# RMSNorm with SiLU on one core: five loads and 174 semaphore increments ahead of the entry barrier, and a scratch transfer on ScalarE's queue

## The chip, the core and the metric

The kernel runs on one core of a Trainium2 chip. A core has TensorE (PE), VectorE (DVE), ScalarE (ACT), GpSimd (POOL) and SyncE (SP), each with an instruction stream of its own, and 16 DMA engines that move data between the chip's memory (HBM, "DRAM" in the code) and the on-chip memory SBUF. The metric is device microseconds of one execution. The kernel before takes 161.42 us, the median of three runs (161.13 to 161.73).

## The reference

```python
batch, seq, dim = 16, 1024, 512          # x: float32, 33.6 MB; gamma: ones(512); eps: 1e-5
rms = np.sqrt(np.mean(x ** 2, axis=-1, keepdims=True) + eps)
x_norm = x / rms * gamma
return (x_norm * (1.0 / (1.0 + np.exp(-x_norm)))).astype(np.float32)
```

There are 16,384 rows of 512 numbers. Each row is divided by its root mean square, multiplied by gamma and passed through SiLU. 33.55 MB are read and 33.55 MB are written.

## The kernel before

**Tiling.** The rows lie over 128 partitions, 128 rows for each. They are computed in place in `xb`, a ring of 100 rows for each partition, in 32 chunks of `cn = 4` rows. The 128 rows are cut into 12 loads and 11 stores, given as (first row, rows): the loads are (0,4), (4,4), (8,8), five of 16 rows, (96,4), (100,12), (112,12) and (124,4); the stores are (0,16), (16,8), (24,8), four of 16 rows, (96,4), (100,12), (112,8) and (120,8). A load or store of n rows moves one run of n x 2 KB for every partition, so 4 rows are 8 KB runs, 1 MB in all.

**The DMA order.** All loads (L121) and stores (L127) are issued by SyncE, in an order written out by hand: nine loads, which fill the ring, then three stores, then the last three loads, then eight stores. The last three loads reuse the ring's first 28 rows, so each waits for the semaphore of a store. A store waits on `s_swish` until its chunks are computed. At the end SyncE waits (L238) for the stores that nothing has waited for yet.

**The entry barrier.** The framework puts a block ahead of the kernel body (L255 in the profile): GpSimd fills four constants, every engine executes a DRAIN, and all meet at a barrier of semaphores. Two more such rounds follow (L66, where the tile context is closed). The kernel takes the first `early = 2` loads out of the body and inserts them into SyncE's entry stream ahead of its DRAIN, so that the transfers start while the engines still meet.

**One chunk.** ScalarE waits for the chunk's load (L167), squares two rows with a running sum (L170, each followed by an instruction that reads the accumulator), and squares the other two into PSUM (L177). VectorE sums these two (L205). GpSimd adds eps (L151) and raises to the power -0.5 (L158). VectorE multiplies four rows by that and by gamma (L216). ScalarE applies SiLU in place to the four rows (L189), two chunks after it squared them.

**Gamma.** GpSimd clears `gamma4` (L146), ScalarE issues a DMA (L193) that puts gamma into one partition of each quarter, ScalarE loads its activation table (L196), and VectorE spreads gamma over the partitions (L229).

Of the kernel before, what the change touches and what calls it, by code (L numbers as in the profile page):

```python
# [9 lines left out]
def kernel(  # L10
# [7 lines left out]
    nc = tc.nc  # L18
    P = nc.NUM_PARTITIONS
    AF = mybir.ActivationFunctionType  # L20
    ALU = mybir.AluOpType
    fp32 = mybir.dt.float32
# [12 lines left out]
    order += [("store", t) for t in range(3)]  # L35
    order += [("load", i) for i in range(loads.index((100, 12)), len(loads))]
    order += [("store", t) for t in range(3, len(stores))]
    early = 2
    cn = 4
    n_sq = 2  # L40

# [26 lines left out]
    def sbuf(name, shape, dt=fp32):  # L68
        return nc.alloc_sbuf_tensor(name, shape, dt).ap()
# [10 lines left out]

    ld = [nc.alloc_semaphore(f"ld{t}") for t in range(len(loads))]
    st = [nc.alloc_semaphore(f"st{t}") for t in range(len(stores))]
    s_gld = nc.alloc_semaphore("s_gld")
    s_zero = nc.alloc_semaphore("s_zero")
    s_half = nc.alloc_semaphore("s_half")
# [9 lines left out]
    def need(ins, sem, value):  # L95
        return ins.wait_op(sem, value, "sem-ge")

    def dram(ap, piece):
        a, n = piece
        g = max(g for g in range(len(groups)) if first[g] <= a)  # L100
        r = a - first[g]
        assert r + n <= groups[g], piece
        rows = ap[P * first[g] : P * (first[g] + groups[g])]
        return rows.rearrange("(p n) d -> p n d", n=groups[g])[:, r : r + n, :]

    def buf(piece):
        a, n = piece
        at = a % ring
        assert at + n <= ring, piece
        return xb[:, at : at + n, :]  # L110
# [3 lines left out]
    def load(i):  # L114
        a, n = loads[i]
        for u, (c, m) in enumerate(stores):
            over = c + ring < a + n and a < c + m + ring
            if over and u not in stored_by_sync:
                nc.sync.wait_ge(st[u], 16)
                stored_by_sync.add(u)  # L120
        return nc.sync.dma_start(  # L121
            out=buf(loads[i]), in_=dram(xf, loads[i])
        ).then_inc(ld[i], 16)

    def store(t):
        need(
            nc.sync.dma_start(out=dram(of, stores[t]), in_=buf(stores[t])),  # L127
            s_swish, ends[t],
        ).then_inc(st[t], 16)

    entry = nc.main_func.blocks[0].instructions
    here = nc.cur_bb.bb.instructions
    for t in range(early):
        ins = load(t).ins
        assert here[-1] is ins or here[-1].name == ins.name
        here.pop()
        at = next(
            i for i, other in enumerate(entry)
            if other.engine == mybir.EngineType.SP
            and isinstance(other, mybir.InstDrain)  # L140
        )
        entry.insert(at, ins)
    for what, t in order[early:]:
        load(t) if what == "load" else store(t)

    nc.gpsimd.memset(gamma4, 0.0).then_inc(s_zero, 1)  # L146
    nc.gpsimd.memset(neg_half, -0.5).then_inc(s_half, 1)  # L147
    nc.gpsimd.wait_ge(s_half, 1)
    for k in range(K):
        need(  # L150
            nc.gpsimd.tensor_scalar(  # L151
                out=aeps[:, k, :], in0=ms[:, k, :], scalar1=eps_f, scalar2=None,
# [6 lines left out]
                out=rstd[:, k, :], in0=aeps[:, k, :], in1=neg_half, op=ALU.pow  # L159
# [25 lines left out]
    def swish(k):  # L185
# [3 lines left out]
            nc.scalar.activation(out=rows, in_=rows, func=AF.Silu), s_norm, k + 1  # L189
        ).then_inc(s_swish, 1)  # L190

    need(
        nc.scalar.dma_start(out=gamma4[0:P:32, :], in_=gamma.partition_broadcast(4)),  # L193
        s_zero, 1,
# [79 lines left out]
```

## Time and profile before

| | before |
|---|---|
| median of 3 runs | 161.42 us (161.13 to 161.73) |
| the profiled execution | 161.94 us, of which the profile's span is 160.6 us |
| busy DVE, ACT, POOL | 124.5, 129.6, 65.4 us |
| SyncE's DMA queue (q1) | 67.11 MB, 98.1% of 16 engines' span |
| ScalarE's DMA queue (q10) | 8 packets, 0.01 MB |
| instruction queue (q14) | 4 packets in the span, 0.03 MB |
| last store | issued at 140.45 us, landed at 160.58 us |

The span runs from the first instruction of the program (SyncE's first load, at 0.00) to its last (SyncE's last wait); the 1.3 us between the span and the execution's time lie outside the program. The profile lists the engines' instructions; SyncE's loads and stores are shown by the instant at which they are issued, and the 16 DMA engines that carry them have rows of their own. Besides the instructions, the trace holds a record of every DMA packet (queue, start, duration, size) and of every increment of a semaphore; where a time below is given from these records, it says so.

### The profile page before, as it was taken

The numbers are of one execution on the slowest core, as the hardware profiler recorded it, in microseconds if no ns is written. First come the engines' busy times: TensorE is split into PE (matmuls) and PEld (weight loads), VectorE is DVE, ScalarE is ACT, GpSimd is POOL, SyncE is SP. The second block draws the span as 40 slices with busy tenths as digits, with TensorE's granted clock in tenths as the row PEclk, the third lists the DMA queues.
The fourth block names the chain that finished last, engine by engine and source line by source line (L and its number), as shares of the span: only waits on it lengthen the run. The fifth ranks groups of instructions, "written<-read, shape, count | busy, mean of one in ns | idle before, by whom it ended". The sixth has DMA issues, their size and how long they took to land.

```text
span 160.6 us, 503 instructions
## 1 busy us (share of the span) xinstructions
DVE 124.5 (78%) x162; ACT 129.6 (81%) x193; POOL 65.4 (41%) x70
## 2 busy tenths in 40 slices
DVE  0287959999999999999999999999999999400000
ACT  1939959999999999999999999999999994700000
POOL 1053545555555555555555555555555555000000
DMA  7999999999999999999999999999999999899993
GB/s 263 449 465 392 498 416 392 481 432 392 453 449 400 424 404 369 459 424 392 426 453 447 410 435 433 435 465 408 424 475 408 400 490 416 369 451 437 428 420 139
DMA packets 3324, 67.15 MB, mean 418 GB/s; under 512 B 372, under 2 KB 372, under 8 KB 376
## 3 DMA queue, kind: packets, MB, share of 16 engines
q1 hardware_dynamic: 3312, 67.11, 98.1%
q14 instruction: 4, 0.03, 0.0%
q10 hardware_dynamic: 8, 0.01, 0.0%
HBM read 33.56 MB, written 33.55 MB: 418 GB/s over the span
## 4 chain that ended last, share of the span: by engine, by line
ACT 63%; DMA 12%; issue 7%; DVE 4%; SPq 0%; ACTq 0%
ACT xb L189 25%; ACT junk L170 22%; ACT sq L177 16%; DMA xb<-in_x_dram 12%; DVE xb L216 3%; DVE ms L205 1%; SPq L121 0%; ACTq L167 0%
## 5 line engine op out<-in xcount | busy, mean ns | idle before, releaser
L216 DVE SCALAR_TENSOR_TENSOR xb<-xb,rstd,gamma_sb 128x512 f32<-128x512 f32 x128 | 87.3, 745 | 0.0
L189 ACT ACTIVATE xb<-xb 128x2048 f32<-128x2048 f32 x32 | 60.9, 1903 | 2.8 <-DVE xb L216 2.8
L205 DVE TENSOR_REDUCE ms<-sq 128x2 f32<-128x1024 f32 x32 | 39.2, 1225 | 14.0 <-ACT sq L177 10.6
L151 POOL TENSOR_SCALAR aeps<-ms 128x4 f32<-128x4 f32 x32 | 20.6, 645 | 65.6 <-DVE ms L205 65.6
L158 POOL TENSOR_TENSOR rstd<-aeps,neg_half 128x4 f32<-128x4 f32 x32 | 44.0, 1376 | 2.7
L170 ACT ACTIVATE junk<-xb 128x512 f32<-128x512 f32 x64 | 37.2, 582 | 4.5 <-DMA xb<-in_x_dram 4.5
L177 ACT ACTIVATE sq<-xb 128x1024 f32<-128x1024 f32 x32 | 32.2, 1005 | 0.0
L170 ACT ACTIVATION_READ_ACCUMULATOR junk<-xb 128x1 f32 x64 | 11.9, 186 | 0.0
L196 ACT ACT_TABLE_LOAD x1 | 1.3, 1283 | 3.6 <-issue 3.6
L146 POOL MEMSET gamma<- 128x512 f32 x1 | 0.5, 525 | 1.5 <-POOLq L66 1.5
L229 DVE STREAM_SHUFFLE gamma_sb<-gamma 128x512 f32<-128x512 f32 x1 | 0.7, 720 | 0.0
L255 POOL MEMSET const-float32-0.0<- 128x1 f32 x1 | 0.1, 99 | 0.2 <-issue 0.2
L255 POOL MEMSET const-bfloat16-1.0<- 128x1 bf16 x1 | 0.1, 102 | 0.0
L255 POOL MEMSET const-uint8-127<- 128x1 uint8 x1 | 0.1, 102 | 0.0
L147 POOL MEMSET neg_half<- 128x4 f32 x1 | 0.1, 102 | 0.0
L255 POOL MEMSET const-float32-1.0<- 128x1 f32 x1 | 0.1, 98 | 0.0
L229 DVE LOAD_MASK_SELECT gamma_sb<-gamma x1 | 0.0, 15 | 0.0
## 6 DMA issues: line engine op xcount, KB each, us to landing
xb<-in_x_dram SPq DMA_DIRECT2D x5, 4096.0 KB, 38.5
out_dram<-xb SPq DMA_DIRECT2D x5, 4096.0 KB, 36.3
out_dram<-xb SPq DMA_DIRECT2D x4, 2048.0 KB, 30.2
xb<-in_x_dram SPq DMA_DIRECT2D x2, 3072.0 KB, 18.2
xb<-in_x_dram SPq DMA_DIRECT2D x4, 1024.0 KB, 12.3
out_dram<-xb SPq DMA_DIRECT2D x1, 3072.0 KB, 25.0
xb<-in_x_dram SPq DMA_DIRECT2D x1, 2048.0 KB, 10.2
out_dram<-xb SPq DMA_DIRECT2D x1, 1024.0 KB, 29.7
```

The costliest lines, as they stand in the source:

```text
L146: nc.gpsimd.memset(gamma4, 0.0).then_inc(s_zero, 1)
L147: nc.gpsimd.memset(neg_half, -0.5).then_inc(s_half, 1)
L151: nc.gpsimd.tensor_scalar(out=aeps[:, k, :], in0=ms[:, k, :], scalar1=eps_f, scalar2=None, op0=ALU.add,),
L158: nc.gpsimd.tensor_tensor(out=rstd[:, k, :], in0=aeps[:, k, :], in1=neg_half, op=ALU.pow),
L170: acc = nc.scalar.activation(out=junk[n % 2], in_=xb[:, at + j, :], func=AF.Square, scale=inv_d**0.5, accum_out=ms[:, k, j : j + 1],)
L177: square = nc.scalar.activation(out=sq[k % 2], in_=xb[:, at : at + n_sq, :], func=AF.Square, scale=inv_d**0.5,)
L189: nc.scalar.activation(out=rows, in_=rows, func=AF.Silu), s_norm, k + 1
L196: nc.scalar.preload_act_table_set("silu_and_others")
L205: nc.vector.tensor_reduce(out=ms[:, k, 0:n_sq], in_=sq[k % 2], op=ALU.add, axis=mybir.AxisListType.X,),
L216: ins = nc.vector.scalar_tensor_tensor(out=row, in0=row, scalar=rstd[:, k, j : j + 1], in1=gamma_sb, op0=ALU.mult, op1=ALU.mult,)
L229: nc.vector.stream_shuffle(gamma_sb, gamma4, [0] * 32), s_gld, 16
L255: nc = _bacc.Bacc("TRN2", target_bir_lowering=False, num_devices=1)
```

## The change

- Five loads instead of two, (0,4), (4,4), (8,8), (16,16) and (32,16), are inserted ahead of SyncE's first DRAIN.
- 76 instructions on ScalarE, 48 on VectorE and 50 on GpSimd, each of which only adds 1 to a new semaphore `s_ahead`, are inserted ahead of the first DRAIN of their engine. Nothing waits for `s_ahead`. In GpSimd's stream the four constants stand before them.
- A small SBUF tensor `blank` (128 partitions x 16 numbers) is cleared by GpSimd before `gamma4`. ScalarE issues a transfer of it to a DRAM tensor `scratch`, 64 bytes for each partition, ahead of gamma's transfer. SyncE waits for its landing after it has issued its last store.

```diff
-    early = 2
+    early = 5
...
+    scratch = nc.dram_tensor("scratch", [P, 16], fp32, kind="Internal").ap()
+    blank = sbuf("blank", [P, 16])
+    s_blank = nc.alloc_semaphore("s_blank")
+    s_scratch = nc.alloc_semaphore("s_scratch")
...
-    for t in range(early):
-        ins = load(t).ins
+    def ahead(engine, ins):
         assert here[-1] is ins or here[-1].name == ins.name
         here.pop()
         at = next(
             i for i, other in enumerate(entry)
-            if other.engine == mybir.EngineType.SP
-            and isinstance(other, mybir.InstDrain)
+            if other.engine == engine and isinstance(other, mybir.InstDrain)
         )
         entry.insert(at, ins)
+    for t in range(early):
+        ahead(mybir.EngineType.SP, load(t).ins)
+    s_ahead = nc.alloc_semaphore("s_ahead")
+    for queue, engine, count in (
+        (nc.scalar, mybir.EngineType.Activation, 76),
+        (nc.vector, mybir.EngineType.DVE, 48),
+        (nc.gpsimd, mybir.EngineType.Pool, 50),
+    ):
+        for _ in range(count):
+            ahead(engine, queue.nop(nofuse=True).then_inc(s_ahead, 1).ins)
     for what, t in order[early:]:
         load(t) if what == "load" else store(t)
+    nc.sync.wait_ge(s_scratch, 16)
+    nc.gpsimd.memset(blank, 0.0).then_inc(s_blank, 1)
     nc.gpsimd.memset(gamma4, 0.0).then_inc(s_zero, 1)
...
+    need(nc.scalar.dma_start(out=scratch, in_=blank), s_blank, 1).then_inc(
+        s_scratch, 16
+    )
     need(
         nc.scalar.dma_start(out=gamma4[0:P:32, :], in_=gamma.partition_broadcast(4)),
```

## Prediction, made before the changed kernel ran

> **What bounds the kernel now.** I read the page's DMA rows first.
>
> ```profile
> span 160.6 us, 503 instructions
> DMA  7999999999999999999999999999999999899993
> q1 hardware_dynamic: 3312, 67.11, 98.1%
> q14 instruction: 4, 0.03, 0.0%
> q10 hardware_dynamic: 8, 0.01, 0.0%
> ```
>
> The 16 DMA engines are full in every slice but the first and the last; no compute engine comes near that (ACT, the busiest, has 129.6 us). A table by stage shows the two open ends, its last columns being the DMA share and GB/s:
>
> ```profile
> core 0: us, DVE busy (x) ACT busy (x) POOL busy (x), PEclk, DMA share, GB/s
> 0.00:1.00 1.00, 0.00 (x0) 0.00 (x0) 0.19 (x4) 1.00 0.03 8
> 1.00:4.00 3.00, 0.00 (x0) 0.43 (x1) 0.56 (x2) 1.00 0.99 347
> ...
> 157.00:158.40 1.40, 0.00 (x0) 0.00 (x0) 0.00 (x0) 1.00 0.52 222
> 158.40:160.60 2.20, 0.00 (x0) 0.00 (x0) 0.00 (x0) 1.00 0.07 30
> ```
>
> Nothing moves for the first microsecond, and in the last 2.2 us the share is 0.07: of 16 engines about one works. All 16 carry the same bytes, so one DMA engine is late, and the kernel waits for it. SyncE's own waits agree: what ends last is a store's landing.
>
> ```profile
> SPq L127 <- ACT xb L189: 93.2, 10, 24.7
> SPq L121 <- DMA out_dram<-xb: 37.5, 3, 28.5
> SPq L238 <- DMA out_dram<-xb: 19.7, 4, 7.2
> ```
>
> Compute has slack. By the records the last store is issued at 140.45 and its first part lands at 157.90; the store before it begins to land at 153.03, so the last one could be issued 12.6 us later with the queue still full.
>
> **Where the late engine loses its time.** The packet records give each engine's position against the median at every landing. At 21 us the largest lag is 0.3. Four 8 KB packets of the instruction queue, at 40.44, 44.10, 77.16 and 119.84, sit on engines amid the data. After the one at 44.10 (0.33 us) the same engine's next 32 KB read takes 1.88 us where 1.22 is normal: that engine is then 0.88 late, the last of all. It grows to 1.5 at 65 us and to 2.25 at 102 us, at the two places where reads change to writes: a laggard still reads while the others write, and at each place the records hold one 8 KB read of 1.02 or 1.03 us for a normal 0.31. The engine of the packets at 40.44 and 119.84 reads 0.55 late, takes almost nothing at the changes, and ends 1.1 late. The packet at 77.16 costs 0.3, among stores.
>
> **Part 1, the 174 increments.** They shift every later instruction of their stream, and with it the instant at which the stream's next 8 KB of code are fetched. At 64 bytes an instruction (an estimate: ScalarE starts 64 rows before 40.44 and 189 before 119.84, and 125 is near 8192/64 = 128) I assign 40.44 and 119.84 to ScalarE, 44.10 to VectorE (50 rows started, some queued) and 77.16 to GpSimd (53). With 76, 48 and 50 more ahead, ScalarE's fetch falls among the increments; VectorE's and GpSimd's fall there or just behind the barrier. All three then come before about 8 us. 128 instructions on, ScalarE fetches near 77 and VectorE near 110 us, both after the change to stores at 63; GpSimd's stream ends first. So five fetches stand for four, but none amid the 32 KB reads.
>
> What an early fetch costs: below, nothing (the first microsecond has idle engines, and the first 8 KB reads take 0.4 to 1.0 us anyway, so that some of it may vanish); above, 0.97 (0.31 plus the 0.66 behind the fetch at 44.10). Gamma's 2 KB packets at 6.3 to 7.1 us, amid 8 and 16 KB reads, left no next packet more than 0.1 longer, so I take 0.31 + 0.07 = 0.38, nearest in time and size. VectorE's DMA engine then is 0.38 late at 63 and 100, under the 0.55 that went unpunished (0.1 for both changes), and adds 0.5 near 110 (0.55 at 119.84): 1.0. ScalarE's is 0.38 + 0.39 (as at 77.16) = 0.8, and may meet the change at 100. Lag at the end 1.1 for 2.25: **-1.15 us**.
>
> The Trainium skill (Runtime: NRT & Kernel Launch, Instruction fetch mechanics) speaks against this: it has instructions come in 16 KiB blocks of 256, at a cost that is mostly hidden. The packets here are 8192 bytes, and the trace hides them from the compute engines only. By the page the sum for this part would be 0.
>
> **Part 2, the time that the increments take.** One EVENT_SEMAPHORE lasts 17 ns on ACT and POOL and 21 on DVE; from one to the next instruction the records have up to 92, 79 and 112. So 76 take 1.3 to 7.0 us, 48 take 1.0 to 5.4, 50 take 0.9 to 4.0. SyncE needs about 2.1 us for five issues (0.33 to 0.44 each) and a DRAIN. The barrier, left at 1.83 us now, is left between 3 and 8 us. I take 6, since an increment is nearest the back-to-back rows. SyncE's other 18 issues are queued behind it, but the five loads are 48 rows, which land at 31 us: no DMA engine runs dry (two loads would have ended at 7 us). ScalarE's start is behind it too:
>
> ```profile
> 2.46 1.08 ACTq L193 DMA_DIRECT2D gamma<-in_gamma_dram  x1
> ...
> 4.86 0.60 ACT L170 ACTIVATE junk<-xb 128x512 f32<-128x512 f32 x1
> ...
> 12.21 0.60 ACT L170 ACTIVATE junk<-xb 128x512 f32<-128x512 f32 x1 [2.64 <-DMA xb<-in_x_dram]
> ...
> 21.92 0.60 ACT L170 ACTIVATE junk<-xb 128x512 f32<-128x512 f32 x1 [1.62 <-DMA xb<-in_x_dram]
> ```
>
> The first square moves from 4.86 by at most 6.2 (barrier) plus 1.08 (a second issue), to 12.2. The waits of 2.64 and 1.62 absorb 4.3; at most 3 to 5 us, gamma's later landing included, reach the steady part. The 12.6 us ahead of the last store cover them: **0 us**. Without cover it would be those 3 to 5.
>
> **Part 3, the scratch transfer.** 128 runs of 64 bytes are 8 packets and a completion on each DMA engine, all 16 alike, so it adds to the bound. Bounds: 9 x 9 ns (a 4-byte completion packet) = 0.08 us, and 9 x 84 ns (gamma's 2 KB packet) = 0.76. Nothing speaks for less than zero, except that a disturbed start might re-order the reads: I allow -0.1. 64 bytes is nearer to 4: **+0.2 us**. The small clear (0.1 us) and SyncE's wait (28 ns, for a transfer over 130 us before) lie behind other work: 0.
>
> The Trainium skill (DMA: Bandwidth & Descriptors, Rules for kernel authors) says that a transfer under 64 KB is mostly overhead; its table has 0.68 us for 4 KB, by which this term would be 0.7, an estimate of mine from a row for another queue.
>
> **Sum.** 161.94 - 1.15 + 0.2 = 161.0 for a profiled execution. That one lies 0.52 over the median of the runs; the same step gives 161.42 - 0.95 = 160.5, and I say 160.6, as runs below the profiled one may hold a smaller lag.
>
> **Rivals.** *A, the lag comes back:* the early fetch costs its upper 0.97 on VectorE's DMA engine, which is then over 0.88 late at both changes (+0.62, +0.75) and gains 0.5 at 110: 2.8 for 2.25, and with 0.2 for scratch 162.2. It decides from an early lag of about 0.8. For it: lags of 0.3 from the first loads do persist to 60 us. Against: gamma's packets left no such mark. *B, half:* ScalarE's DMA engine, 0.8 late after 77, is caught at 100 (+0.75), or scratch is near its upper 0.76; the end moves by -0.7 + 0.2 to -1.15 + 0.76, that is 160.9 to 161.0, or the fetches do not move at all (no code boundary there): 161.6. *C, all of it:* the early fetches vanish in the startup, lag 0.5, 161.42 - 1.75 + 0.1 = 159.8.
>
> **Chances.** Main 0.35 (160.2 to 160.9), C 0.13, B 0.30, A 0.22. The range 159.7 to 162.3 takes in A's and C's times. A measurement of this kernel tells about 0.5% (0.8 us) from no change: faster means under 160.6. Half and more of the main case and all of C are faster, B lies within, most of A is slower (with the long end of scratch): 0.43, 0.34, 0.23.
>
> **What would show it.** In the profile after: four or five q14 packets, three of them before 8 us; a last stretch at a share near 0.07 that is about 1 us long; q10 up by 144 packets and no gap in the DMA row; the first square between 7 and 12 us, and the last store over 5 us ahead of the queue. I am wrong if the lag at 60 us is already 0.8, if q10's packets hold the engines for over 0.5 us each, or if the DMA row shows a slice with idle engines.

## The result, and the profile after

| | before | after |
|---|---|---|
| median of 9 runs each, side by side | 161.47 us (161.13 to 161.73) | 162.10 us (161.82 to 162.33) |
| the profiled execution | 161.94 us, span 160.6 | 162.10 us, span 160.8 |

The ratio is 1.0031, with a 95% interval of 1.0018 to 1.0043. The changed kernel is slower, by 0.5 us going by the ratio and by 0.6 us going by the medians. That is inside the predicted range and inside the 0.5% that the prediction called no change, but the forecast of 160.6 us had the wrong sign. The profiled execution of the kernel before lies above all nine of its runs, so the two spans, 0.2 us apart, understate the difference; the part on the prediction comes back to it. Execution and span differ by about 1.3 us in every profile of this case, so nothing outside the program moved.

The page of the changed kernel, its span and its DMA rows:

```profile
span 160.8 us, 680 instructions
DMA  7999999999999999998999999999999999899993
q1 hardware_dynamic: 3312, 67.11, 98.0%
q10 hardware_dynamic: 152, 0.02, 0.1%
q14 instruction: 5, 0.04, 0.1%
```

The DMA row is as full as before. q10 has grown by the 144 packets that were foreseen, and q14, which carries the engines' code, has five packets for four. The table by stage (columns: DVE, ACT and POOL busy, granted clock, DMA share, GB/s) shows the same open end:

```profile
157.00:158.40 1.40, 0.00 (x0) 0.00 (x0) 0.00 (x0) 1.00 0.66 281
158.40:160.80 2.40, 0.00 (x0) 0.00 (x0) 0.00 (x0) 1.00 0.06 27
```

At a share of 0.06 one engine of 16 is working: the last stretch has not shrunk to the foreseen 1 us. In this text the *lag* is the time of the last of the 16 engines' completions of the last store, less their median. It was 160.58 - 158.34 = 2.24 us in the profiled execution before, and it is 160.74 - 158.43 = 2.31 after. The median engine is done at the same time in both; what differs between kernels is how late the last engine is.

The records name neither the stream that a code packet belongs to nor its DMA engine. The streams are told apart by the experiments below; packets are put on one engine where one starts within some 10 ns of the other's end. By these records the code packets lie at 8.35 and 10.11 us (ScalarE and GpSimd), **27.26 (VectorE)**, 82.60 (ScalarE) and **118.50 (VectorE)**. So VectorE's first fetch was not early. Its timeline, with the start and length of each instruction and the idle time ahead of it in brackets, shows where the stream stood:

```profile
14.21 1.23 DVE L224 TENSOR_REDUCE ms<-sq 128x2 f32<-128x1024 f32 x1 [14.21 <-ACT sq L193]
22.20 0.01 DVE L248 LOAD_MASK_SELECT gamma_sb<-gamma  x1 [6.77 <-DMA gamma<-in_gamma_dram]
22.20 0.72 DVE L248 STREAM_SHUFFLE gamma_sb<-gamma 128x512 f32<-128x512 f32 x1
```

VectorE had nothing to do until gamma landed at 22.17 us. The reading, tested below, is that its next 8 KB of code begin a little behind that wait, so that its sequencer asked for them only after the wait was over. The packet came 5 us after the wait's end, in the middle of the 32 KB reads.

Gamma itself was late because of ScalarE's queue:

```profile
6.61 0.35 ACTq L208 DMA_DIRECT2D scratch<-blank  x1
7.07 3.54 ACTq L212 DMA_DIRECT2D gamma<-in_gamma_dram  x1
10.64 1.28 ACT L215 ACT_TABLE_LOAD   x1 [10.64 <-issue]
11.94 0.60 ACT L186 ACTIVATE junk<-xb 128x512 f32<-128x512 f32 x1
```

Issuing gamma took 3.54 us where it took 1.08 before, and the first square starts at 11.94 instead of 4.86. SyncE's waits, by line, show what the delay cost later:

```profile
SPq L131 <- ACT xb L205: 110.9, 10, 32.2
SPq L125 <- DMA out_dram<-xb: 27.1, 3, 18.1
SPq L257 <- DMA out_dram<-xb: 9.1, 2, 4.8
```

SyncE now waits longer for compute (110.9 us for 93.2) and shorter at the end for landings (9.1 for 19.7): the last store is issued at 151.03 us instead of 140.45. The store before it begins to land at about 153, so some 2 us of the 12.6 us of slack are left, and the queue still never runs dry.

### The profile page after: what moved, and what is told of

It reads as the page before. It is cut to its first block, busy times and chain, and to the rows that moved or that the text cites. A ratio compares the mean times of both kernels' runs of the same rounds, so it can differ in the third digit from the quotient of the medians.

```text
span 160.8 us, 680 instructions
## 1 busy us (share of the span) xinstructions
DVE 124.4 (77%) x162; ACT 129.3 (80%) x193; POOL 65.4 (41%) x71
## 4 chain that ended last, share of the span: by engine, by line
ACT 71%; DMA 9%; DVE 6%; issue 3%; POOL 0%; POOLq 0%
ACT xb L205 33%; ACT junk L186 22%; ACT sq L193 16%; DMA gamma<-in_gamma_dram 9%; DVE xb L235 5%; DVE ms L224 1%; DVE gamma_sb L248 0%; POOL gamma L162 0%; POOL blank L161 0%; POOLq L66 0%
## 5 line engine op out<-in xcount | busy, mean ns | idle before, releaser
L215 ACT ACT_TABLE_LOAD x1 | 1.3, 1283 | 10.6 <-issue 10.6
```

Of the source, the lines that this page charges most:

```text
L215: nc.scalar.preload_act_table_set("silu_and_others")
```

## The experiments

The theory after the result: two of VectorE's fetches now fall amid the data where there was one, both are carried by the same DMA engine, and each makes that engine 0.7 to 0.95 us later, so the kernel ends later. Rivals: the scratch transfer costs it; the later start of compute costs it; another engine's fetches do.

### One part at a time

**The scratch transfer alone** (no increments, `early = 2`):

```diff
+    scratch = nc.dram_tensor("scratch", [P, 16], fp32, kind="Internal").ap()
...
+    nc.sync.wait_ge(s_scratch, 16)
+    nc.gpsimd.memset(blank, 0.0).then_inc(s_blank, 1)
...
+    need(nc.scalar.dma_start(out=scratch, in_=blank), s_blank, 1).then_inc(
+        s_scratch, 16
+    )
```

> The kernel before plus the scratch transfer alone. Theory L (the latest DMA engine sets the end, and where the code fetches fall sets that engine): the number of fetches stays four, all of them later by as much as compute is late (some 7 to 10 us, since gamma waits behind the scratch packets, one of them for each 1.2 us packet of SyncE's queue); VectorE's still falls amid the 32 KB reads, so the time is that of before plus 0.1 us for 9 small packets on each DMA engine: 161.5 to 161.7 us. Theory S (the scratch transfer and the late compute cost the 0.6 us): 162.0 to 162.2 us.

Measured: 161.64 us for 161.60, ratio 1.0006 (0.9995 to 1.0017). The fetches stay near their places of before (40.44, 44.11, 73.79 and 119.81 us) and the lag at the end is 1.67. A scratch packet of 64 bytes holds its engine for 11 ns; eight of them and a completion of 9 ns are about 0.1 us for each engine. The transfer by itself costs nothing that these runs can tell.

**Everything but the scratch transfer** (against the changed kernel):

```diff
...
-    nc.sync.wait_ge(s_scratch, 16)
...
-    need(nc.scalar.dma_start(out=scratch, in_=blank), s_blank, 1).then_inc(
-        s_scratch, 16
-    )
```

> The changed kernel without the scratch transfer. Theory L: five fetches, among them two early ones at 8 to 10 us, GpSimd's amid the 32 KB reads (near 18 us, since its stream then waits for the first sums) and VectorE's at about 110 us on a DMA engine that is late already: 161.8 to 162.1 us. Theory S: as before, 161.4 to 161.5 us. Compute should be only some 5 us later than before, and the last store issued near 145 us.

Measured: 162.26 us for 161.60, ratio 1.0041 (1.0026 to 1.0057), lag 2.41. The loss is there without scratch. Gamma landed at 16.22 us, and VectorE's fetch moved along with it, to 21.20 us: a first sign that the gamma wait sets its time.

**The five early loads alone**:

```diff
-    early = 2
+    early = 5
```

> Five loads ahead of the barrier, no increments, no scratch. Both theories: no DMA engine was idle there and no code boundary moves on ScalarE, VectorE or GpSimd, so 161.4 to 161.6 us. A rival, that the later barrier costs or gains by itself (1.2 us): 160.5 or 162.5.

Measured: 161.61 us for 161.60, ratio 1.0002 (0.9991 to 1.0012); four fetches, at 40.41, 44.24, 77.22 and 120.91 us; lag 2.00. Nothing.

**Five loads and ScalarE's 76 increments alone**:

```diff
-    early = 2
+    early = 5
...
+        (nc.scalar, mybir.EngineType.Activation, 76),
+        (nc.vector, mybir.EngineType.DVE, 0),
+        (nc.gpsimd, mybir.EngineType.Pool, 0),
```

> Five loads and the 76 increments on ScalarE alone, no scratch: the barrier is as late as in the changed kernel (about 6.4 us), but VectorE's and GpSimd's streams are those of before. Theory L: ScalarE fetches near 8 and 80 us, VectorE near 47 us amid the 32 KB reads (0.9 us), GpSimd near 80 us: four fetches, the lag of before, 161.3 to 161.8 us. If the late barrier by itself is the cause, as the run without scratch, whatever that is.

Measured: 161.42 us for 161.60, ratio 0.9987 (0.9978 to 0.9997). ScalarE's fetches moved from 40 and 120 us to 8.78 and 77.13, which settles whose they are. VectorE's one fetch came at 49.02, GpSimd's at 82.15. The lag is 1.67. If anything this part helps. Compute starts late here too (gamma landed at 16.67 us, the last store was issued at 145.55), so a start later by that much costs nothing by itself.

**The changed kernel with none of VectorE's increments**:

```diff
-        (nc.vector, mybir.EngineType.DVE, 48),
+        (nc.vector, mybir.EngineType.DVE, 0),
```

> The changed kernel with VectorE's 48 increments taken out; ScalarE's 76, GpSimd's 50, the five loads and the scratch transfer stay. Theory L: VectorE's stream is that of before, so it fetches once, near 50 us, amid the 32 KB reads (lag 0.9 to 1.0 at 60 us, 1.7 behind the change at 63), and the fetch near 118 us is gone: the end's lag is 1.6 to 2.0 and the time 161.4 to 161.7 us. A rival, that the increments cost by their number or by the later barrier: 161.9 to 162.1 us.

Measured: 161.65 us for 161.67, ratio 0.9997 (0.9985 to 1.0009). The loss is gone, though scratch, 126 increments and the late gamma are all still there. Its page and the last 2 us of its table by stage:

```profile
span 160.2 us, 632 instructions
q14 instruction: 4, 0.03, 0.0%
```

```profile
158.80:160.80 2.00, 0.00 (x0) 0.00 (x0) 0.00 (x0) 1.00 0.02 8
```

Four code packets, one of them VectorE's (53.87 us), and a share of 0.02 where one late engine over the whole 2 us would be 0.06: the lag is 1.64.

**Five loads and VectorE's 48 increments alone**, the counterpart:

```diff
-    early = 2
+    early = 5
...
+        (nc.scalar, mybir.EngineType.Activation, 0),
+        (nc.vector, mybir.EngineType.DVE, 48),
+        (nc.gpsimd, mybir.EngineType.Pool, 0),
```

> Five loads and VectorE's 48 increments alone. The runs so far put a fetch of VectorE's code at 0.9 to 0.95 us of its DMA engine amid reads (0.31 for the packet, 0.6 that the next read is longer by) and 0.65 to 0.75 amid stores. Theory F (the second fetch of VectorE's code is the whole loss): two such fetches, the first behind VectorE's wait for gamma, the second near 112 us; lag at the end 2.3 to 2.5 and 162.2 to 162.4 us. If the increments on ScalarE or GpSimd are needed for the loss: 161.6 to 161.9 us.

Measured: 162.34 us for 161.70, ratio 1.0038 (1.0025 to 1.0050), lag 2.35.

```profile
span 160.8 us, 551 instructions
q14 instruction: 5, 0.04, 0.1%
```

```profile
158.80:160.80 2.00, 0.00 (x0) 0.00 (x0) 0.00 (x0) 1.00 0.04 16
```

These 48 instructions are the whole loss. VectorE's fetches lie at 17.47 us, with the engine's next 32 KB read at 1827 ns for 1213, and at 108.81, with its next store packet at 1564 ns for 1213. Together with the experiment before this settles the cause: VectorE's increments are enough for the loss, and without them it is gone. That they act by the second fetch rests on the packet records: in all four runs with two fetches of VectorE and the order of before, the latest engine's lag rises where the second one lies, from 1.58 to 2.42 us in the changed kernel, 1.71 to 2.50 without scratch, 1.62 to 2.40 here and 1.58 to 2.47 in the next run. No run has increments on VectorE that are too few for a second fetch.

### When the first fetch comes, and what it costs there

**64 increments on VectorE instead of 48, without scratch.** 16 more instructions put the boundary ahead of the gamma wait:

```diff
...
-        (nc.vector, mybir.EngineType.DVE, 48),
+        (nc.vector, mybir.EngineType.DVE, 64),
```

> The changed kernel without scratch, and with 64 increments on VectorE for 48. Theory L with the reading that VectorE's sequencer stood at its wait for gamma just short of the code boundary: the boundary now falls among the increments, so VectorE's fetch comes by 10 us, amid 8 and 16 KB reads, and its DMA engine is 0.6 late at 60 us for 1.06, under what is punished at 63 us. The second fetch comes 16 rows earlier than at 112.6, near 100 us. Lag at the end 1.0 to 1.6, time 160.8 to 161.5 us; if the change to stores at 100 us catches it, 161.8. If the reading is wrong, a fetch stays near 21 us and the time is 162.2 us.

Measured: 162.33 us for 161.67, ratio 1.0040 (1.0025 to 1.0055). The fetch did come early, at 9.54 us, so the boundary was read rightly. The time was missed: the early fetch was no cheaper. By 22 us its engine was 1.02 behind; the second one, at 100.18 us, fell on 8 KB reads (the next took 907 ns for 309), and the lag at the end is 2.39. Where the boundary lies behind the wait, the fetch followed the wait's end by 4.9 to 5.6 us in four runs whose waits ended at 11.86, 16.25, 21.10 and 22.20 us. So the wait for gamma explains when the fetch came, and not what it cost: amid reads VectorE's fetch costs about 0.9 us early as well as late.

**Smaller reads around VectorE's fetch at 44 us** (the kernel before, its load (64,16) cut in two). If the cost were one packet's worth of a 32 KB read, 16 KB reads would halve it:

```diff
-    loads = [(0, 4), (4, 4), (8, 8), (16, 16), (32, 16), (48, 16), (64, 16), (80, 16)]
+    loads = [(0, 4), (4, 4), (8, 8), (16, 16), (32, 16), (48, 16)]
+    loads += [(64, 8), (72, 8), (80, 16)]
```

> The kernel before with its load of rows 64 to 79 cut in two of 8 rows, so that VectorE's fetch at 44 us falls amid 16 KB reads for 32 KB. Theory L: the read behind the fetch loses 0.3 us for 0.66, the DMA engine is 0.5 to 0.6 late at 60 us for 0.9, and takes nothing at the change at 63 us. Lag at the end 0.9 to 1.1 (ScalarE's DMA engine), time 160.7 to 161.0 us. If lags do not set the end, or the change does not punish by lag: 161.4 to 161.7 us.

Measured: 161.74 us for 161.67, ratio 1.0007 (0.9993 to 1.0020), so the expected gain did not come. The next 16 KB read took 1274 ns for 613, and the engine was still 1.04 late at 60 us. **Both neighbouring loads cut**, so that the fetch falls on 16 KB reads for certain:

```diff
+    loads = [(0, 4), (4, 4), (8, 8), (16, 16), (32, 16), (48, 8), (56, 8)]
+    loads += [(64, 8), (72, 8), (80, 16)]
```

> As the run before it, and the load of rows 48 to 63 is cut in two of 8 rows as well, where ScalarE's fetch at 40 us falls. Theory L: ScalarE's DMA engine is 0.3 late at 60 us for 0.5, and the lag at the end is 0.8 to 1.0: 160.6 to 160.9 us. If smaller reads cost by themselves (16 KB at 0.611 us against 32 KB at 1.215, 8 ns for each pair, 0.1 us in all), 0.1 us above the run before it.

Measured: 161.62 us for 161.67, ratio 0.9996 (0.9985 to 1.0008). Again no gain: the next 16 KB read took 1240 ns for 614, 0.63 us longer. The size of the read does not set the cost.

### Where the fetch meets writes

In all records VectorE's fetch made the next packet 0.58 to 0.66 us longer amid reads and 0.35 to 0.42 amid stores. So the kernel before should gain if its fetch at 44 us fell on writes. **The first three stores are moved ahead of load (64,16)**, where they write from 41 to 60 us:

```diff
-    order = [("load", i) for i in range(loads.index((100, 12)))]
+    order = [("load", i) for i in range(loads.index((64, 16)))]
     order += [("store", t) for t in range(3)]
-    order += [("load", i) for i in range(loads.index((100, 12)), len(loads))]
+    order += [("load", i) for i in range(loads.index((64, 16)), len(loads))]
```

> The kernel before with the first three stores moved ahead of the loads of rows 64 and on, so that the DMA engines write from 41 to 60 us and read from 60 to 102 us. Same bytes, same number of changes between reads and writes. Theory F: VectorE's fetch at 44 us falls among stores (0.7 us for 0.95), and no DMA engine is over 0.7 late at the change from reads to writes at 41 us, so nothing is punished there; the end's lag is 1.0 to 1.2 for 1.7 to 2.0 and the time 160.7 to 161.1 us. Compute waits up to 2 us more for rows 64 and on, of 12.6 us slack. If the punishment at the change is not one for lag, the time stays at 161.4 to 161.7 us.

Measured: 161.06 us for 161.70, ratio 0.9952 (0.9937 to 0.9966), lag 1.06. **One load earlier still**, with (48,16) cut so that the change from reads to writes falls between the halves:

```diff
+    loads = [(0, 4), (4, 4), (8, 8), (16, 16), (32, 16), (48, 8), (56, 8)]
+    loads += [(64, 16), (80, 16)]
...
+    order = [("load", i) for i in range(loads.index((56, 8)))]
```

> As the run before it, but the stores start at 36 us: the load of rows 48 to 63 is cut in two and they go between the halves. ScalarE's fetch at 40 us then falls among stores too (0.45 us for 0.65). Theory F: lag at the end 0.8 to 1.0, time 160.5 to 160.9 us, if compute, which needs row 56 at about 62 us, is not held up by more than its slack.

Measured: 160.97 us for 161.70, ratio 0.9949 (0.9936 to 0.9962), just above what was expected. Its page and the end of its table by stage:

```profile
span 159.6 us, 505 instructions
DMA  7999999999999999999989999999999999899996
q14 instruction: 4, 0.03, 0.0%
```

```profile
157.00:158.80 1.80, 0.00 (x0) 0.00 (x0) 0.00 (x0) 1.00 0.68 291
158.80:160.80 2.00, 0.00 (x0) 0.00 (x0) 0.00 (x0) 1.00 0.00 0
```

The last digit of the DMA row is 6 for 3, and the queues move nothing in the last stretch: the last landing follows the median one by 0.83 us. These two are the fastest versions here, ahead of both kernels and not told apart from each other.

By the packet records two things changed at once for VectorE's DMA engine. Its fetch makes it 0.60 and 0.65 us later, for 0.92 in the profile of before. And it is not yet late when the reads change to writes at 41 and 36 us, and takes no more at 100 us, where that profile has rises of 0.6 and 0.7 at the two changes. It ends 0.40 and 0.55 late; what ends last is now ScalarE's engine, with its fetches at 41.96 and 122.56 us (lag 1.06), 40.55 and 122.36 us (0.83). So the gain is shown for the order of loads and stores as a whole; the cheaper fetch is the smaller part of it, and no run separates the two.

**The same order in the changed kernel**:

```diff
-    order = [("load", i) for i in range(loads.index((100, 12)))]
+    order = [("load", i) for i in range(loads.index((64, 16)))]
...
+    order += [("load", i) for i in range(loads.index((64, 16)), len(loads))]
```

> The changed kernel, whole, with its first three stores moved ahead of the loads of rows 64 and on (writes from 41 to 60 us). VectorE's first fetch comes near 27 us, amid reads, so its DMA engine is 0.9 to 1.0 late at the change from reads to writes at 41 us. If a DMA engine that is so late is punished there as at 63 us (0.5 to 0.75), the lag is 1.5 behind the change, 2.2 at the end, and the time 162.0 to 162.3 us. If the punishment belonged to the 8 KB load at 60 to 63 us, the lag stays at 0.95 until VectorE's second fetch and ends at 1.7: 161.5 to 161.8 us.

Measured: 163.43 us for 161.86, ratio 1.0107 (1.0084 to 1.0131); its profiled execution, 162.63, is the fastest of its runs. This lies outside both expected ranges and does not decide what it was meant to:

```profile
DMA  7999999999999799999989999999999999899996
```

The 7 in the fourteenth slice is an idle queue. Compute is about 10 us late here, so the third store is issued at 55.46 us, after the transfers ahead of it have ended, and the engines stand for about 1 us. That idle time also let the late engine catch up (the lag at the end is 0.85), so the two effects can't be separated. It does show what the slack of the other runs was worth: where the order leaves none, compute's delay costs time at once. In the same run a lag of 0.84 crossed the change from reads to writes at 41 us without growing (0.83).

## Why the prediction was right or wrong

**What bounds the kernel: right.** In the runs with the order of before, the lag of the last DMA engine follows the number of VectorE's fetches: 1.4 to 2.0 with one amid the reads (2.24 in the one profiled execution of before), 2.3 to 2.4 with two. With VectorE's one fetch amid writes the lag is 0.8 to 1.1, and another engine sets it.

**The lag that the sum started from, 2.25: not that of the median.** In ten profiles of other kernels with this order, an execution's time less its lag is 159.7 to 160.0 us, and in the profile of before it is 159.7. By that the median of 161.47 goes with a lag of 1.4 to 1.8 (an estimate). The profiled execution of before, 0.47 us slower, has the rest from the change to writes at 100 us, where its lag rose by 0.74; in nine of the other profiles it rose by -0.05 to 0.31 there, and in the tenth a fetch falls on it. The prediction took its whole 1.15 off the median and gave back 0.1; a lag of 1.1 at the end would have saved 0.3 to 0.7.

**"All three then come before about 8 us": failed for VectorE.** ScalarE's and GpSimd's came at 8.35 and 10.11. VectorE's came at 27.26, because I let its stream run on behind the barrier without looking at where it stops: at the wait for gamma. The case that the prediction excluded, a fetch amid the 32 KB reads, is what happened.

**"What an early fetch costs: 0.38": failed.** This is the term that turned the sign. Packet and longer next packet together, fetches amid reads cost 0.57 to 0.69 for GpSimd and ScalarE and 0.89 to 0.99 for VectorE, early or late. Gamma's 2 KB packets were the wrong row to take it from; the upper bound, 0.97 from VectorE's own fetch at 44 us, was about right, as the run with 64 increments shows (0.31 + 0.58 at 9.54 us). The engine was then not under the 0.55 that "went unpunished", so the rise at 63 us came as well. The sign that the prediction had named, a lag of 0.8 already at 60 us, is there: 0.96. On VectorE's DMA engine the terms are:

| step, on VectorE's DMA engine | predicted, us | measured, us |
|---|---|---|
| first fetch | 0.38 | 0.90 (27 us, 0.31 + 0.59; lag 0.96 at 60 us) |
| the two changes from reads to writes | 0.1 | 0.6 (lag 1.53 at 65 us, 1.58 at 112) |
| second fetch | 0.5 near 110 | 0.8 at 118.50 (lag 2.4 at 122) |
| lag at the end | 1.1 | 2.31 |

Rival A had the time (162.2 us, measured 162.10) and nearly the price (0.97). Its fetch was not early, though, and its second penalty at 100 us did not come. That its time came out is in part luck: its lag at the end, 2.8, was 0.5 too long, and the 2.25 that it was set against was too long by about as much.

**Second fetches "near 77" and "near 110": right in kind.** They were at 82.60 and 118.50, later since compute was later. ScalarE's engine did not set the end, and where its increments stood alone the kernel lost nothing (0.9987).

The Trainium skill (Runtime: NRT & Kernel Launch, Instruction fetch mechanics) has code come in 16 KiB blocks at a cost that is mostly hidden. In these runs the packets are 8192 bytes, and VectorE's stream has 50 rows started at its fetch without the increments and 178 at its second fetch with them, 128 apart. The cost is hidden from VectorE, but not from the DMA engine that carries the packet, and here that engine sets the end.

**Part 2, 0 us: right, by less than it said.** The barrier was left at 6.40 us (6 foreseen) and the first square began at 11.94 (at most 12.2). But compute was 10.6 us later at the last store and not 3 to 5, as gamma's landing was mis-sized:

| | gamma landed, us | last store issued, us |
|---|---|---|
| before | 8.14 | 140.45 |
| scratch alone | 11.15 | 140.39 |
| after without scratch | 16.22 | 145.10 |
| after | 22.17 | 151.03 |

Scratch's packets were ahead of gamma's on ScalarE's queue. The records have them from 10.11 to 18.78 us, eight for each engine, about one for each of the large reads of SyncE's queue. The Trainium skill (DMA: Bandwidth & Descriptors, Queues, rings and completion order) says that a DMA engine goes round its queue rows in turn. The trace agrees on the turns; the section's turn is a packet of about 9 to 17 descriptors, and here it was mostly one 64-byte record. The step failed because it priced the barrier and the issue, and not the queue that gamma waits in. The cover of 12.6 us held with about 2 us to spare, and the run without VectorE's increments, which had nearly the same delay (last store issued at 149.87), lost nothing.

**Part 3, +0.2: within its bounds.** The packets hold an engine for 0.1 us, and the ratio 1.0006 covers both 0.2 and nothing.

**What stays open.** Between 60 and 65 us, where the last 8 KB reads are followed by stores, the latest engine's lag rises by 0.5 to 0.75 in all eleven profiles with this order; at 100 us it sometimes rises and sometimes not (1.51 to 1.57 after, 1.50 to 2.24 in the profiled execution before), and at 41 us of the last experiment it did not. A rule "the late engine is punished at each change from reads to writes" is therefore not shown. Why VectorE's fetches cost more than ScalarE's and GpSimd's is not shown either; only that they do.

## What to carry to other kernels

In a kernel that is bound by DMA, an instruction is not free because its engine idles: code is fetched by the same DMA engines as the data, so count the instructions of each stream, find where the boundaries lie, and look for the wait that the sequencer stands at just before them. Price a fetch from one of the same stream's own fetches, at the place where it will lie. Where one engine ends late, look at the order of loads and stores too: here an order that put stores where the fetch falls, and kept a late engine away from the change to writes, gained 0.5%. No way of moving the fetch among the reads that was tried here gained as much.

## What the runs showed of the hardware that was not expected

- A code packet of 8192 bytes takes 0.31 to 0.33 us on its DMA engine, and that engine's next packet is longer too. Amid reads: 0.58 to 0.66 us longer after VectorE's, 0.28 to 0.38 after ScalarE's, 0.26 to 0.30 after GpSimd's. Amid stores: 0.35 to 0.42, 0.11 to 0.20 and 0.08 to 0.09. After VectorE's it is the same for reads of 8, 16 and 32 KB (0.60, 0.58 to 0.66, 0.59 to 0.66).
- In all four runs with two fetches of VectorE and the order of before, the second fell on the same DMA engine as the first, and so did ScalarE's in both kernels, so that a stream's fetches add up on one engine; the engine's packets are back to back, and its lag stays as it is to the end unless the queue runs dry.
- Instructions that only increment a semaphore follow each other by 67.6 ns on ScalarE, 92.7 on VectorE and 78.3 on GpSimd in the changed kernel, although one lasts 17 to 21 ns. Where ScalarE alone has them, it is 77.6.
- A transfer of 8 KB costs its DMA engines 0.1 us each and can hold up a small transfer behind it on its own queue by 6 us (gamma's landing, 16.22 to 22.17), when another queue has large packets waiting.
